# ConvFFN entry of a two-layer decoder trunk: matmuls of the first block alternate between gate and up, the norm's factor is taken earlier, and two operand tiles lie 384 bytes further on

## The chip, the cores and the metric

The kernel runs on one core of a Trainium2 chip. The metric is the device time of one execution in microseconds; the median of the runs is given, and beside it one execution that the hardware profiler recorded. Engines are called as the profile calls them: PE is TensorE (matmuls; PEld are its weight loads), DVE is VectorE, ACT is ScalarE, POOL is GpSimd, SP is SyncE, which issues the DMAs.

## The reference

Two layers over 256 tokens of width 1024. Each layer is attention, then a gated ConvFFN; cut to what matters here:

```python
def hybrid_layer(x, ...):
    h = rms_norm(x, ln1)
    proj = h @ w_in                       # 14 pieces, three kinds of attention heads
    ...
    x = x + jnp.concatenate([o_a, o_b, o_c], axis=-1) @ w_out
    return x + conv_ffn(rms_norm(x, ln2), w_gate, w_up, conv_w, conv_b, w_down)

def conv_ffn(h, w_gate, w_up, conv_w, conv_b, w_down):   # D_FF = 2816
    g = h @ w_gate
    u = h @ w_up
    g = conv_general_dilated(g, conv_w, ...) + conv_b    # causal, depthwise, width 3
    return (jax.nn.silu(g) * u) @ w_down

def rms_norm(x, g):
    return x * lax.rsqrt(jnp.mean(x * x, axis=-1, keepdims=True) + EPS) * g
```

## The kernel before

**Precision.** Every large product is made of three matmuls (`mm3`, L216): both operands are split into a high part and the rest (`hi`, `lo` for weights; `hTh`, `hTl` for the normed input; `oh`, `ol` for the attention output; `aTh`, `aTl` for the FFN's inner activations), and high x high, rest x high and high x rest are summed in PSUM. All of them here have 128 x 128 weights and 256 moving columns, one per token. The weight split (`split_next`, L194) costs one instruction on ACT (`hi`, L202) and one on DVE (`lo`, L203) per 128 x 1024 piece; the pieces come in a fixed order from the DMA queue of SP through three buffers `raw`, and their split parts go through a ring of seven buffers. `weights(ahead)` returns the next split piece and first splits so many pieces further on.

**The output projection and the entry to the ConvFFN.** The projection `w_out` is summed in eight PSUM accumulators (`ps_out`); its last two of eight pieces run behind one another (`down(acc, oT, 6, 8, ...)`), and as each of the eight output slices j is done, DVE adds it to the residual `xT` (L905), ACT makes `hTh[j]` and the square of the slice, DVE makes `hTl[j]`, and POOL adds the square into `sqs`. The FFN then goes in 22 blocks m of 128 inner channels; a block has 24 matmuls for gate and 24 for up, eight slices k of three matmuls each. The gain of the norm is in `hTh`; its factor R, one number per token, is applied later, to the gate product (`gate`, L935) and to the silu (L951). `norm2` (L919) makes R: `sqs` is split in two (`sqh` on ACT, `sql` on DVE), two matmuls with ones (`onesr`) sum it over the partitions into `ps_R`, and `rsqrt` (L221) makes R of the sum by one DVE, two ACT and three DVE instructions.

**What sets the order.** The DMA queue runs in written order throughout. In the loop over m, DVE, ACT and POOL are in written order too, `tc.manual_schedule(engines={ET.DVE, ET.Activation, ET.Pool})`; PE is ordered by a scheduler. At m = 0 the kernel before calls `weights()` twice with six pieces ahead, so that four further pieces (for blocks 2 and 3) are split before `norm2` is written. The gate and up accumulators of blocks take turns over three pairs of PSUM banks: a pair is used again three blocks later. The inner products then go to `w_down` (`ps_dn`) in the same manner, 22 x 24 matmuls.

**Where operands lie.** In a partition's memory each weight slice of `hi` and `lo` starts at a multiple of 512 bytes. `hTh`, `hTl`, `aTh`, `aTl`, `sqh` and `sql` start 448 bytes past one (a slice of 256 columns is 1024 bytes, so all slices do), `oh` and `ol` 64 bytes past one, `onesr` 448 past one. In the input projection (`ps_in`) the roles are exchanged: the moving columns are those of `hi` and `lo`, the weights those of `hTh` and `hTl`. In the piece of 256 columns (chunk 7) the moving operand therefore starts at a multiple of 512 and the weights 448 past one, which is the same distance, 64, as that of `oh` to its weights.

Of the kernel before, what the change touches and what calls it, by code (L numbers as in the profile page):

```python
# [23 lines left out]
D = 1024  # L24
HD = 64
DFF = 2816
NM = DFF // P
DEPTH = 2
EPS = 1e-6
# [29 lines left out]
CN = [len(c) for c in CHUNKS]  # L59
# [52 lines left out]
def emit(ctx, tc, a):  # L112
    nc = tc.nc
    V, A, T, G = nc.vector, nc.scalar, nc.tensor, nc.gpsimd

    cst = ctx.enter_context(tc.tile_pool(name="cst", bufs=1))
    lay = ctx.enter_context(tc.tile_pool(name="lay", bufs=2))
    wr = ctx.enter_context(tc.tile_pool(name="wr", bufs=3))
# [9 lines left out]
    ident = con[:, O_ID:O_ID + P]  # L128
    xT = cst.tile([P, 8, S], F32, name="xT")
    ones = cst.tile([P, P], F32, name="ones")  # L130
    onesr = cst.tile([P, P], F32R, name="onesr")
    G.memset(ones, 1.0)
    G.memset(onesr.bitcast(F32), 1.0)
    blk = [cst.tile([P, 16, 32], F32, name=f"blk{i}") for i in range(2)]
# [12 lines left out]
    def f(t):  # L147
        return t.bitcast(F32)
# [7 lines left out]
    for L in range(DEPTH):  # L156
        for c in range(8):
            n = CN[c]
# [17 lines left out]
    splits = []  # L176
    after = []

    raw0 = wr.tile([P, 4 * 2 * CN[0]], F32, name="raw0", bufs=1)

    def fetch(u):
        if u in raws:
# [8 lines left out]
        for load in extras.get(u, ()):  # L191
            load()

    def split_next():  # L194
        u, h = parts[len(ready)]
        src, n, np_ = stream[u]
        if h == 0:
            fetch(u)
        hi = wr.tile([P, 1024], F32R, tag="hi", name="hi", bufs=SPN)
        lo = wr.tile([P, 1024], F32R, tag="lo", name="lo", bufs=SPN)  # L200
        r = raws[u][:, h * n:(h + 1) * n]
        splits[:] = [A.activation(out=hi[:, :n], in_=r, func=ACTF.Copy),  # L202
                     V.tensor_tensor(out=lo[:, :n], in0=r, in1=f(hi[:, :n]), op=ALU.subtract)]  # L203
        ready.append((hi, lo))

    def weights(ahead=AHEAD):
        i = taken[0]
        taken[0] += 1
        while len(ready) < min(i + 1 + ahead, len(parts)):
            with ExitStack() as st:  # L210
                for ins in after:
                    st.enter_context(tc.issue_after(ins.ins))
                split_next()
        return ready[i]

    def mm3(out, lh, ll, rh, rl, start, stop, skip=False):  # L216
        T.matmul(out, lhsT=lh, rhs=rh, start=start, stop=False, skip_group_check=skip)  # L217
        T.matmul(out, lhsT=lh, rhs=rl, start=False, stop=False, skip_group_check=skip)  # L218
        T.matmul(out, lhsT=ll, rhs=rh, start=False, stop=stop, skip_group_check=skip)  # L219

    def rsqrt(out, ss, n, tmp=None):  # L221

        v, w, q = tmp or [sml.tile(list(out.shape), F32, tag=f"rs_{i}", name=f"rs_{i}") for i in "vwq"]

        V.tensor_scalar(v, ss, 1.0 / n, EPS, ALU.mult, ALU.add)
        A.activation(out=w, in_=v, func=ACTF.Ln)
        A.activation(out=w, in_=w, func=ACTF.Exp, scale=-0.5)
        V.tensor_tensor(q, w, w, ALU.mult)
        V.scalar_tensor_tensor(q, q, -0.5, v, ALU.mult, ALU.mult)
        V.scalar_tensor_tensor(out, q, 1.5, w, ALU.add, ALU.mult)  # L230
# [54 lines left out]
        nc.sync.dma_start(out=con[:, o0:o1], in_=a["con"][:, o0:o1])  # L285

    pools = []
    masks = cst.tile([P, 4, 384], BF16, name="masks")

    def load_masks(i):  # L290
        raw = pools[0].tile([P, 768], F32, tag="pr", name="raw_m", bufs=4)
# [53 lines left out]
    for L in range(DEPTH):  # L345
# [564 lines left out]
        with ExitStack() as ph:  # L910
            ff = ph.enter_context(tc.tile_pool(name=f"ff{L}", bufs=2, reuse_waits="tile"))

            aTh = ff.tile([P, 96 + NM * S], F32R, tag="aTh", name="aTh", bufs=1)[:, 96:].rearrange("p (m s) -> p m s", m=NM)
            aTl = ff.tile([P, NM, S], F32R, tag="aTl", name="aTl", bufs=1)
            cw = sm[:, O_CW:O_CW + 66].rearrange("p (m w) -> p m w", w=3)
            cb = sm[:, O_CB:O_CB + 22]
            R = lay.tile([P, S], F32, tag="R", name="R", bufs=1)

            def norm2():  # L919

                ps = bank("pt", "ps_R")
                sq, = sqs2
                sh, sl = [ff.tile([P, S], F32R, tag=n, name=n, bufs=1) for n in ("sqh", "sql")]
                A.copy(sh, sq)
                V.tensor_tensor(sl, sq, f(sh), ALU.subtract)
                for i, s_ in enumerate((sh, sl)):
                    T.matmul(ps[:, :S], lhsT=onesr, rhs=s_, start=i == 0, stop=i == 1)
                v, w, q = [ff.tile([P, S], F32, tag=n, name="R_" + n, bufs=3) for n in ("gr", "cy", "cs")]
                rsqrt(R, ps[:, :S], D, (v, w, q))

            gates, ups, ys, ss = {}, {}, {}, {}

            def gate(m):
                gr = ff.tile([P, S], F32, tag="gr", name="gr", bufs=3)
                V.tensor_tensor(gr, gates.pop(m), R, ALU.mult)  # L935
                return gr

            def conv(m, gr):
                y = ys[m] = ff.tile([P, S], F32, tag="cy", name="cy", bufs=3)
                A.activation(out=y, in_=gr, func=ACTF.Identity, scale=cw[:, m, 2:3], bias=cb[:, m:m + 1])  # L940

            def taps(m, gr):
                y = ys[m]
                for j in (1, 2):
                    V.scalar_tensor_tensor(out=y[:, j:], in0=gr[:, :S - j], scalar=cw[:, m, 2 - j:3 - j], in1=y[:, j:],  # L945
                                           op0=ALU.mult, op1=ALU.add)

            def silu(m):
                s_ = ss[m] = ff.tile([P, S], F32, tag="cs", name="cs_", bufs=3)
                A.activation(out=s_, in_=ys[m], func=ACTF.Silu)  # L950
                G.tensor_tensor(s_, s_, R, ALU.mult)  # L951

            def product(m):
                V.tensor_tensor(ys[m], ups.pop(m), ss.pop(m), ALU.mult)


            with tc.manual_schedule(engines={ET.DVE, ET.Activation, ET.Pool}):
                for m in range(NM + 2):
                    a_, b_, c_ = 2 <= m <= NM, m >= 2, m < NM
                    if a_:  # L960
                        gr = gate(m - 1)
                    if b_:
                        product(m - 2)
                    if c_:
                        gates[m], ups[m] = [bank((("acc", "s"), ("o", "m"))[m % 3 == 1][i], "ps_gu")[:, :S] for i in range(2)]
                        ws = [weights()]
                    if a_:
                        conv(m - 1, gr)
                    if b_:
                        A.copy(aTh[:, m - 2], ys[m - 2])  # L970
                    if a_:
                        taps(m - 1, gr)
                    if b_:
                        V.tensor_tensor(aTl[:, m - 2], ys[m - 2], f(aTh[:, m - 2]), ALU.subtract)
                    if c_:
                        ws.append(weights())
                    if a_:
                        silu(m - 1)
                    if c_:
                        for ps, (hi, lo) in zip((gates[m], ups[m]), ws):  # L980
                            for k in range(8):
                                cs = slice(k * P, (k + 1) * P)
                                mm3(ps, hi[:, cs], lo[:, cs], hTh[:, k], hTl[:, k], k == 0, k == 7)
                    if m == 0:
                        after.clear()
                        norm2()
                    if m == 1:
                        gr = gate(0)
                        conv(0, gr)
                        taps(0, gr)  # L990
                        silu(0)
                    if m in (10, 13) and L + 1 < DEPTH:
                        T1, T2 = rope_tables(L + 1, (m // 13,), None if m == 10 else (T1, T2))
            acc = [bank(t, "ps_dn") for t in ("pt", "pt", "o", "m")]
            for m in range(NM - 4):
                if m == 8 and L + 1 < DEPTH:
                    tc.keep_in_program_order(A.preload_act_table_set(TABLES))
                down(acc, (aTh, aTl), m, m + 1, NM - 1)
            if L + 1 < DEPTH:
                sqs1 = []  # L1000

            def new_x(j, ps):
                if L + 1 < DEPTH:
# [50 lines left out]
```

## Time and profile before

| | |
|---|---|
| median of 3 runs (656.75, 650.28, 649.35) | 650.28 us |
| the profiled execution | 650.62 us |
| its span, first to last instruction | 648.9 us |
| PE busy | 637.4 us (98%) |
| PE weight loads busy | 597.0 us (92%) |
| DVE busy | 473.6 us (73%) |
| ACT busy | 413.7 us (64%) |
| granted TensorE clock, mean | 1.000 |

Matmuls are pipelined: each is shown as lasting some 0.28 us, but the next starts after 0.11 to 0.12 us, so the pace is read from the starts. The entry to the ConvFFN of the first layer is at 146 to 160 us, that of the second at 464 to 478 us. A window of time counts the instructions that run in it, so one that began before its start is counted too.

### The profile page before, as it was taken

What the parts mean: (1) busy time and instruction counts of PE and PEld (TensorE: products, weight loads), DVE (VectorE), ACT (ScalarE), POOL (GpSimd) and SP (SyncE); (2) the same over time, 40 slices, a digit from 0 to 9 for tenths busy, and PEclk for the clock granted to TensorE, in tenths of its full rate; (3) what the DMA queues carried; (4) which work ended last, traced back from release to release, by engine and by line L of the source; (5) the groups of instructions that cost most, each with busy time, mean ns of one, the idle gap of its engine ahead of it and who ended that gap; (6) DMA issues with size and microseconds to landing.
All of it is one profiled execution on the core that took longest, in us unless ns stands there. A gap on an engine that the chain in (4) does not pass through costs nothing.

```text
span 648.9 us, 12854 instructions
## 1 busy us (share of the span) xinstructions
PE 637.4 (98%) x5074; PEld 597.0 (92%) x5074; DVE 473.6 (73%) x1024; ACT 413.7 (64%) x834; POOL 107.4 (17%) x123
## 2 busy tenths in 40 slices
PE   8999999999999999999999999999999999999997
PEld 8889878789999999999997887788999999999997
DVE  6679987758898888744487898685779888886432
ACT  7477899766775555543475789897757655555320
POOL 3301000012324422200120000010303222221000
PEclk9999999999999999999999999999999999999999
DMA  8853263434465555554664523333156655555501
GB/s 318 361 182 145 66 212 114 145 131 148 179 234 214 192 195 190 182 203 158 231 227 146 179 66 131 131 130 130 66 195 220 234 195 196 195 196 195 191 5 66
DMA packets 19356, 111.84 MB, mean 172 GB/s; under 512 B 2144, under 2 KB 3936, under 8 KB 8288
## 3 DMA queue, kind: packets, MB, share of 16 engines
q1 hardware_dynamic: 19296, 111.02, 48.0%
q8 instruction: 40, 0.66, 0.4%
q14 instruction: 20, 0.16, 0.1%
HBM read 109.97 MB, written 1.05 MB: 171 GB/s over the span
## 4 chain that ended last, share of the span: by engine, by line
PE 81%; DVE 8%; ACT 6%; DMA 2%; issue 2%; POOL 1%; SPq 0%; POOLq 0%; DVEq 0%; ACTq 0%
PE ps_gu L218 12%; PE ps_gu L219 12%; PE ps_gu L217 12%; PE ps_dn L218 6%; PE ps_dn L217 6%; PE ps_dn L219 6%; PE ps_in L217 4%; PE ps_in L218 4%; PE ps_in L219 4%; DVE lo L203 2%; PE ps_p L526 2%; PE ps_o L538 2%; ACT hi L202 2%; PE ps_out L217 2%; PE ps_out L219 2%
## 5 line engine op out<-in xcount | busy, mean ns | idle before, releaser
L203 DVE TENSOR_TENSOR lo<-raw,hi 128x1024 fp32r<-128x1024 f32 (+3 forms) x212 | 241.4, 1147 | 78.3 <-ACT hi L202 77.5
L202 ACT ACTIVATE hi<-raw 128x1024 fp32r<-128x1024 f32 (+3 forms) x212 | 208.3, 994 | 130.3 <-PE ps_gu L218 60.8
L218 PE MATMUL ps_gu<-hTl,hi 128*128 128x256 f32 x704 | 194.7, 277 | 0.2
L217 PE MATMUL ps_gu<-hTh,hi 128*128 128x256 f32 x704 | 194.5, 276 | 0.0
L219 PE MATMUL ps_gu<-hTh,lo 128*128 128x256 f32 x704 | 194.5, 276 | 0.0
L218 PEld LDWEIGHTS ps_gu<-hTl,hi 128*128 128x128 f32 x704 | 132.2, 188 | 0.6 <-DVE hTl L236 0.6
L219 PEld LDWEIGHTS ps_gu<-hTh,lo 128*128 128x128 f32 x704 | 132.2, 188 | 0.0
L217 PEld LDWEIGHTS ps_gu<-hTh,hi 128*128 128x128 f32 x704 | 132.2, 188 | 0.0
L219 PE MATMUL ps_dn<-aTh,lo 128*128 128x256 f32 x352 | 97.2, 276 | 0.0
L217 PE MATMUL ps_dn<-aTh,hi 128*128 128x256 f32 x352 | 97.2, 276 | 0.0
L218 PE MATMUL ps_dn<-aTl,hi 128*128 128x256 f32 x352 | 97.2, 276 | 0.0
L217 PE MATMUL ps_in<-hi,hTh 128*128 128x384 f32 (+3 forms) x256 | 88.2, 347 | 0.5 <-ACT vd L403 0.3
L218 PE MATMUL ps_in<-lo,hTh 128*128 128x384 f32 (+3 forms) x256 | 88.0, 344 | 0.7 <-DVE lo L203 0.7
L219 PE MATMUL ps_in<-hi,hTl 128*128 128x384 f32 (+3 forms) x256 | 88.0, 344 | 0.0
L219 PEld LDWEIGHTS ps_dn<-aTh,lo 128*128 128x128 f32 x352 | 66.1, 188 | 0.0
L217 PEld LDWEIGHTS ps_dn<-aTh,hi 128*128 128x128 f32 x352 | 66.1, 188 | 0.0
L218 PEld LDWEIGHTS ps_dn<-aTl,hi 128*128 128x128 f32 x352 | 66.1, 188 | 0.0
L217 PEld LDWEIGHTS ps_in<-hi,hTh 128*128 128x128 f32 x256 | 47.9, 188 | 6.5 <-issue 1.9
L218 PEld LDWEIGHTS ps_in<-lo,hTh 128*128 128x128 f32 x256 | 48.2, 188 | 4.3 <-DVE lo L203 1.1
L219 PEld LDWEIGHTS ps_in<-hi,hTl 128*128 128x128 f32 x256 | 48.2, 188 | 3.5 <-issue 0.9
L945 DVE SCALAR_TENSOR_TENSOR cy<-gr,sm,cy 128x255 f32<-128x255 f32 x88 | 42.5, 482 | 2.9 <-ACT cy L940 1.3
L217 PE MATMUL ps_out<-oh,hi 128*128 128x256 f32 x128 | 36.6, 289 | 0.0
(321 smaller groups left out, 922.4 us busy)
## 6 DMA issues: line engine op xcount, KB each, us to landing
raw<-w_gu SPq DMA_DIRECT2D x44, 1024.0 KB, 4.8
raw<-w_down SPq DMA_DIRECT2D x22, 1024.0 KB, 4.6
raw<-w_in SPq DMA_DIRECT2D x16, 768.0 KB, 4.5
raw<-w_in SPq DMA_DIRECT2D x8, 1024.0 KB, 4.7
raw<-w_out SPq DMA_DIRECT2D x8, 1024.0 KB, 4.8
w<-cw SPq DMA_DIRECT2D x4, 1024.0 KB, 10.7
raw<-w_in SPq DMA_DIRECT2D x4, 512.0 KB, 3.7
raw<-w_in SPq DMA_DIRECT2D x4, 274.0 KB, 5.1
```

Source lines behind the costliest of these rows:

```text
L202: splits[:] = [A.activation(out=hi[:, :n], in_=r, func=ACTF.Copy), V.tensor_tensor(out=lo[:, :n], in0=r, in1=f(hi[:, :n]), op=ALU.subtract)]
L203: V.tensor_tensor(out=lo[:, :n], in0=r, in1=f(hi[:, :n]), op=ALU.subtract)]
L217: T.matmul(out, lhsT=lh, rhs=rh, start=start, stop=False, skip_group_check=skip)
L218: T.matmul(out, lhsT=lh, rhs=rl, start=False, stop=False, skip_group_check=skip)
L219: T.matmul(out, lhsT=ll, rhs=rh, start=False, stop=stop, skip_group_check=skip)
L526: T.transpose(ps[:, i * P:(i + 1) * P], pr[:, i * P:(i + 1) * P], ident)
L538: return T.matmul(O[k * HD:(k + 1) * HD, qs], lhsT=vs[k][j], rhs=pTs[k][:, 256 * j:256 * j + 256 - 128 * j], start=first and j == 0, stop= ...
L945: V.scalar_tensor_tensor(out=y[:, j:], in0=gr[:, :S - j], scalar=cw[:, m, 2 - j:3 - j], in1=y[:, j:], op0=ALU.mult, op1=ALU.add)
```

## The change

1. In block 0 the products are written k by k, gate and up in turn (`products`), where before all eight k of gate came first and then those of up; later blocks keep gate first.
2. PE is in written order in this loop as well. The two matmuls of `norm2` stand behind the 48 of block 0; the scheduler had put them in between the matmuls of block 1.
3. `norm2` is written around two weight splits: `sqh` right behind the `hi` of the first, `sql` ahead of its `lo`; the first DVE and both ACT instructions of the factor between `hi` and `lo` of the second. Block 0 splits nothing further ahead (`weights(0)`), and later blocks keep four pieces ahead, not six. R is done before any further split.
4. ACT's function table for silu is loaded behind the factor's last ACT instruction, not ahead of the first silu. The gate work of block 0 (`gate(0)`, `conv`, `taps`, `silu`) moves up between the splits of block 1's turn.
5. Tiles are padded: `oh` and `ol` lie 896 bytes further on, which is 384 past a multiple of 512, so that they now start 448 bytes past one. `onesr` now starts at a multiple of 512. Everything else moves by 512 or 1024 bytes, or has no part in these matmuls.

```diff
-    onesr = cst.tile([P, P], F32R, name="onesr")
+    onesr = cst.tile([P, 2 * P], F32R, name="onesr")[:, 16:16 + P]
...
-    raw0 = wr.tile([P, 4 * 2 * CN[0]], F32, name="raw0", bufs=1)
+    raw0 = wr.tile([P, 4 * 2 * CN[0] + 32], F32, name="raw0", bufs=1)
...
-    def split_next():
+    def split_next(between=None):
...
-        splits[:] = [A.activation(out=hi[:, :n], in_=r, func=ACTF.Copy),
-                     V.tensor_tensor(out=lo[:, :n], in0=r, in1=f(hi[:, :n]), op=ALU.subtract)]
+        splits[:] = [A.activation(out=hi[:, :n], in_=r, func=ACTF.Copy)]
+        if between:
+            between()
+        splits.append(V.tensor_tensor(out=lo[:, :n], in0=r, in1=f(hi[:, :n]), op=ALU.subtract))
...
-    masks = cst.tile([P, 4, 384], BF16, name="masks")
+    masks = cst.tile([P, 4 * 384 + 192], BF16, name="masks")[:, :4 * 384].rearrange("p (a b) -> p a b", a=4)
...
+                def total():
+                    A.copy(sh, sq)
+                    V.tensor_tensor(sl, sq, f(sh), ALU.subtract)
+                    for i, s_ in enumerate((sh, sl)):
+                        T.matmul(ps[:, :S], lhsT=onesr, rhs=s_, start=i == 0, stop=i == 1)
+                def first_value():
+                    V.tensor_scalar(v, ps[:, :S], 1.0 / D, EPS, ALU.mult, ALU.add)
+                    A.activation(out=w, in_=v, func=ACTF.Ln)
+                    A.activation(out=w, in_=w, func=ACTF.Exp, scale=-0.5)
+                    A.preload_act_table_set("silu_and_others")
...
+                    split_next(total)
+                after.clear()
+                split_next(first_value)
+                V.tensor_tensor(q, w, w, ALU.mult)
+                V.scalar_tensor_tensor(q, q, -0.5, v, ALU.mult, ALU.mult)
+                V.scalar_tensor_tensor(R, q, 1.5, w, ALU.add, ALU.mult)
...
+            def products(m, ws):
+                order = [(k, i) for k in range(8) for i in range(2)] if m == 0 else [(k, i) for i in range(2) for k in range(8)]
+                for k, i in order:
+                    (hi, lo), cs = ws[i], slice(k * P, (k + 1) * P)
+                    mm3((gates, ups)[i][m], hi[:, cs], lo[:, cs], hTh[:, k], hTl[:, k], k == 0, k == 7)
...
-            with tc.manual_schedule(engines={ET.DVE, ET.Activation, ET.Pool}):
+            with tc.manual_schedule(engines={ET.DVE, ET.Activation, ET.Pool, ET.PE}):
...
+                    if m == 0:
+                        products(0, [weights(0) for _ in range(2)])
+                        norm2()
+                    else:
+                        gr = gate(m - 1) if m <= NM else None
...
+                            ws.append(weights(4))
```

**PE, the start of block 0** in layer 0; `ps_gu_1917` is gate, `ps_gu_1918` up. Before:

```order
L219 MATMUL ps_out_1485<-oh_901,lo_1531 128x256
L217 MATMUL ps_gu_1917<-hTh_91,hi_1612 128x256
L218 MATMUL ps_gu_1917<-hTl_92,hi_1612 128x256
L219 MATMUL ps_gu_1917<-hTh_91,lo_1613 128x256
L217 MATMUL ps_gu_1917<-hTh_91,hi_1612 128x256
L218 MATMUL ps_gu_1917<-hTl_92,hi_1612 128x256
L219 MATMUL ps_gu_1917<-hTh_91,lo_1613 128x256
```

Now:

```order
L221 MATMUL ps_out_1485<-oh_901,lo_1531 128x256
L219 MATMUL ps_gu_1917<-hTh_91,hi_1612 128x256
L220 MATMUL ps_gu_1917<-hTl_92,hi_1612 128x256
L221 MATMUL ps_gu_1917<-hTh_91,lo_1613 128x256
L219 MATMUL ps_gu_1918<-hTh_91,hi_1679 128x256
L220 MATMUL ps_gu_1918<-hTl_92,hi_1679 128x256
L221 MATMUL ps_gu_1918<-hTh_91,lo_1680 128x256
```

Each slice k is now used by six matmuls in a row, so the last slice, k = 7, is first read 42 matmuls after the start, where it was 21.

**PE, the norm's two matmuls.** `hi_1750` and `lo_1751` belong to the gate of block 1. Before:

```order
L218 MATMUL ps_gu_2005<-hTl_92,hi_1750 128x256
L927 MATMUL ps_R_1989<-sqh_1990,onesr_76 128x256
L219 MATMUL ps_gu_2005<-hTh_91,lo_1751 128x256
...
L217 MATMUL ps_gu_2005<-hTh_91,hi_1750 128x256
L927 MATMUL ps_R_1989<-sql_1991,onesr_76 128x256
L218 MATMUL ps_gu_2005<-hTl_92,hi_1750 128x256
```

Now:

```order
L221 MATMUL ps_gu_1918<-hTh_91,lo_1680 128x256
L933 MATMUL ps_R_1967<-sqh_1968,onesr_76 128x256
L933 MATMUL ps_R_1967<-sql_1969,onesr_76 128x256
L219 MATMUL ps_gu_1994<-hTh_91,hi_1750 128x256
L220 MATMUL ps_gu_1994<-hTl_92,hi_1750 128x256
```

Both stand one behind the other between block 0 and block 1, and apart from block 0 nothing else has changed place on PE.

**DVE, from the last `hTl` to the first product.** Before:

```order
L236 SCALAR_TENSOR_TENSOR hTl<-xT,sm,hTh 128x256 x2
L203 TENSOR_TENSOR lo<-raw,hi 128x1024 x4
L925 TENSOR_TENSOR sql<-sqs,sqh 128x256
L225 TENSOR_SCALAR R_gr<-ps_R 128x256
L228 TENSOR_TENSOR R_cs<-R_cy 128x256
L229 SCALAR_TENSOR_TENSOR R_cs<-R_cs,R_gr 128x256
L230 SCALAR_TENSOR_TENSOR R<-R_cs,R_cy 128x256
L203 TENSOR_TENSOR lo<-raw,hi 128x1024 x2
L935 TENSOR_TENSOR gr<-ps_gu,R 128x256
```

Now:

```order
L238 SCALAR_TENSOR_TENSOR hTl<-xT,sm,hTh 128x256 x2
L931 TENSOR_TENSOR sql<-sqs,sqh 128x256
L205 TENSOR_TENSOR lo<-raw,hi 128x1024
L936 TENSOR_SCALAR R_gr<-ps_R 128x256
L205 TENSOR_TENSOR lo<-raw,hi 128x1024
L947 TENSOR_TENSOR R_cs<-R_cy 128x256
L948 SCALAR_TENSOR_TENSOR R_cs<-R_cs,R_gr 128x256
L949 SCALAR_TENSOR_TENSOR R<-R_cs,R_cy 128x256
L955 TENSOR_TENSOR gr<-ps_gu,R 128x256
L205 TENSOR_TENSOR lo<-raw,hi 128x1024
```

Four splits stood ahead of `sql` and six ahead of the first `gr`; now it is none and two.

## Rows read from the trace of the kernel before

**Rows 1.** The page's chain that ended last, shares of the span by engine

```profile
PE 81%; DVE 8%; ACT 6%; DMA 2%; issue 2%; POOL 1%; SPq 0%; POOLq 0%; DVEq 0%; ACTq 0%
```

**Rows 2.** Windows, PE: stretch, us, busy us (count), granted clock, DMA share, GB/s

```profile
155.40:327.30 171.90, 171.90 (x1519) 1.00 0.55 196
473.40:644.90 171.50, 171.50 (x1515) 1.00 0.48 173
138.16:146.39 8.23, 8.23 (x71) 1.00 0.36 127
456.14:464.37 8.23, 8.23 (x71) 1.00 0.37 128
105.03:108.79 3.76, 3.76 (x34) 1.00 0.00 0
113.56:115.81 2.25, 2.25 (x22) 1.00 0.48 127
```

**Rows 3.** Timeline of PE, first layer's entry: start, duration, instruction

```profile
146.52 0.28 PE L217 MATMUL ps_gu<-hTh,hi 128*128 128x256 f32 x1
...
148.99 0.28 PE L217 MATMUL ps_gu<-hTh,hi 128*128 128x256 f32 x1
149.39 0.38 PE L218 MATMUL ps_gu<-hTl,hi 128*128 128x256 f32 x1
149.61 0.28 PE L219 MATMUL ps_gu<-hTh,lo 128*128 128x256 f32 x1
...
152.67 0.28 PE L218 MATMUL ps_gu<-hTl,hi 128*128 128x256 f32 x1
152.89 0.39 PE L927 MATMUL ps_R<-sqh,onesr 128*128 128x256 f32 x1
153.12 0.28 PE L219 MATMUL ps_gu<-hTh,lo 128*128 128x256 f32 x1
...
154.81 0.39 PE L927 MATMUL ps_R<-sql,onesr 128*128 128x256 f32 x1
155.03 0.28 PE L218 MATMUL ps_gu<-hTl,hi 128*128 128x256 f32 x1
...
158.67 0.28 PE L217 MATMUL ps_gu<-hTh,hi 128*128 128x256 f32 x1
```

**Rows 4.** Timeline of PE, second layer: first matmul of block 0 and of block 2

```profile
464.50 0.28 PE L217 MATMUL ps_gu<-hTh,hi 128*128 128x256 f32 x1
...
476.63 0.28 PE L217 MATMUL ps_gu<-hTh,hi 128*128 128x256 f32 x1
```

**Rows 5.** Timeline of DVE, first layer's entry

```profile
147.82 1.51 DVE L236 SCALAR_TENSOR_TENSOR hTl<-xT,sm,hTh 128x256 fp32r<-128x256 f32 x2
149.73 4.68 DVE L203 TENSOR_TENSOR lo<-raw,hi 128x1024 fp32r<-128x1024 f32 x4 [0.40 <-ACT hi L202]
154.34 0.41 DVE L925 TENSOR_TENSOR sql<-sqs,sqh 128x256 fp32r<-128x256 f32 x1
155.23 0.42 DVE L225 TENSOR_SCALAR R_gr<-ps_R 128x256 f32<-128x256 f32 x1 [0.48 <-PE ps_R L927]
160.12 0.42 DVE L935 TENSOR_TENSOR gr<-ps_gu,R 128x256 f32<-128x256 f32 x1
164.86 0.42 DVE L954 TENSOR_TENSOR cy<-ps_gu,cs__2071 128x256 f32<-128x256 f32 x1 [2.31 <-POOL cs__2071 L951]
```

**Rows 6.** Timeline of ACT, first layer's entry

```profile
148.66 3.89 ACT L202 ACTIVATE hi<-raw 128x1024 fp32r<-128x1024 f32 x4
152.45 0.39 ACT L924 CAST sqh<-sqs 128x256 fp32r<-128x256 f32 x1
162.30 1.28 ACT L950 ACT_TABLE_LOAD   x1 [1.12 <-DVE cy L945]
```

**Rows 7.** Timeline of POOL: the last four additions into sqs

```profile
146.47 3.45 POOL L246 TENSOR_TENSOR sqs<-sqs,xsq 128x256 f32<-128x256 f32 x4
```

**Rows 8.** The page's DMA issues: the FFN's weights, KB each, us to landing

```profile
raw<-w_gu SPq DMA_DIRECT2D x44, 1024.0 KB, 4.8
```

More of the change, by code (lines that the diff above doesn't have):

```diff
@@ L923, in norm2 @@
                 sh, sl = [ff.tile([P, S], F32R, tag=n, name=n, bufs=1) for n in ("sqh", "sql")]
[L924 to L927, printed above, removed]
                 v, w, q = [ff.tile([P, S], F32, tag=n, name="R_" + n, bufs=3) for n in ("gr", "cy", "cs")]
-                rsqrt(R, ps[:, :S], D, (v, w, q))
+                def total():
[8 more added lines that the diff above has]
+                    A.preload_act_table_set("silu_and_others")
+                with ExitStack() as st:
+                    for ins in after:
+                        st.enter_context(tc.issue_after(ins.ins))
+                    split_next(total)
[4 more added lines that the diff above has]
+                V.scalar_tensor_tensor(R, q, 1.5, w, ALU.add, ALU.mult)
             gates, ups, ys, ss = {}, {}, {}, {}
@@ L954, in product @@
                 V.tensor_tensor(ys[m], ups.pop(m), ss.pop(m), ALU.mult)
-            with tc.manual_schedule(engines={ET.DVE, ET.Activation, ET.Pool}):
-                for m in range(NM + 2):
[L959 to L964, printed above, removed]
-                        gates[m], ups[m] = [bank((("acc", "s"), ("o", "m"))[m % 3 == 1][i], "ps_gu")[:, :S] for i in range(2)]
[L966 to L983, printed above, removed]
@@ new lines, in products @@
+            def products(m, ws):
[4 more added lines that the diff above has]
+            with tc.manual_schedule(engines={ET.DVE, ET.Activation, ET.Pool, ET.PE}):
+                for m in range(NM + 2):
+                    if m < NM:
+                        gates[m], ups[m] = [bank((("acc", "s"), ("o", "m"))[m % 3 == 1][i], "ps_gu")[:, :S] for i in range(2)]
@@ L984, in emit @@
                     if m == 0:
-                        after.clear()
+                        products(0, [weights(0) for _ in range(2)])
                         norm2()
[L987 to L991, printed above, removed]
+                    else:
+                        gr = gate(m - 1) if m <= NM else None
+                        if m >= 2:
+                            product(m - 2)
+                        ws = []
+                        if m == 1:
+                            conv(0, gr)
+                        if m < NM:
+                            ws.append(weights(4))
+                        if 2 <= m <= NM:
+                            conv(m - 1, gr)
+                        if m >= 2:
+                            A.copy(aTh[:, m - 2], ys[m - 2])
+                        if m <= NM:
+                            taps(m - 1, gr)
+                        if m == 1:
+                            silu(0)
+                        if m >= 2:
+                            V.tensor_tensor(aTl[:, m - 2], ys[m - 2], f(aTh[:, m - 2]), ALU.subtract)
+                        if m < NM:
+                            ws.append(weights(4))
+                        if 2 <= m <= NM:
+                            silu(m - 1)
+                        if m < NM:
+                            products(m, ws)
```

## The prediction

> **What bounds the kernel now.** I read the chain of waits first: 81% of what ended last is PE, so time is won where PE waits or runs slower than it can [rows 1]. Then windows of PE at several places, to get its pace from the count of starts. In the long stretch from the entry of the first layer's ConvFFN to the end of its `ps_dn`, 1,519 matmuls run in 171.90 us; two of them began before the window, so 171.90 / 1,517 = 0.1133 us each, and the second layer's stretch gives the same (171.50 / 1,513) [rows 2]. There PE waits for nothing, so no work of DVE, ACT or the queues counts there. In each layer 70 of the last starts of `ps_out` (one of the 71 was under way) take 8.23 us, 0.1176 us each [rows 2], with the same 256 columns and the granted clock at 1.00 in both, the 2.4 GHz level. So there are two paces without any wait, 0.1133 (fast) and 0.1177 (slow), 4.4 ns apart.
>
> Last I read the entry itself. From the first matmul of block 0 to the first of block 2 there are 98 matmuls, and they take 158.67 - 146.52 = 12.15 us in the first layer [rows 3] and 476.63 - 464.50 = 12.13 in the second [rows 4]. At the fast pace 98 would take 11.11, at the slow one 11.53. The loss sits in three places [rows 3]: `hTl` of slice 7 is awaited (0.40 from 148.99 to 149.39, then 0.22 to the next), and each of the two `ps_R` matmuls costs about 0.2 us in starts that are 0.22 apart; between the first stop and the second PE runs at the slow pace, 26 starts from 149.61 to 152.67, 0.1177 each.
>
> **The change part by part.**
>
> *Slice by slice in block 0.* `hTl` of slice 7 is done at 147.82 + 1.51 = 149.33 [rows 5]. It is now first read 42 matmuls after the block's start, 42 x 0.1133 = 4.8 us, so at 151.0 or later even if PE starts 0.3 us sooner. The wait goes, with 1.6 us to spare. No other slice is nearer: six matmuls last 0.68 to 0.71 us, one turn of DVE's `xT` and `hTl` takes about 0.9, so the margin only shrinks towards k = 7.
>
> *The norm's two matmuls.* They now stand 48 matmuls behind the start, at about 151.7. `sqs` is complete at 146.47 + 3.45 = 149.92 [rows 7]; `sqh` takes 0.39 on ACT, which has one split (0.97) before it instead of four (3.89) [rows 6]; `sql` takes 0.41 on DVE, which has no split before it instead of four (4.68) [rows 5]. So both are there by 150.8, 0.9 us ahead of PE. What is late next is nothing on PE: `R_gr` follows 0.42 us after the second matmul, at 152.2 instead of 155.23; then one split (1.2), then the three further DVE steps at about 0.42; the first `gr` comes near 155.3 instead of 160.12 [rows 5].
>
> *What hangs on the other engines.* Two splits stand behind `gr` that used to stand before it. I estimate the pieces of block 3 done near 158.7 and 162.4; PE reads them at 146.2 + 146 x 0.1133 = 162.7 and 2.7 later. The product of block 0, at 164.86 before, comes near 163.2, and block 3's up, which takes over its bank, starts at 165.4. The table load (1.28 [rows 6]) moves into the time in which ACT waits for R. With four pieces ahead in place of six the `raw` buffers come free later, so their DMAs are issued later. They land in 4.8 us [rows 8] and two blocks, 2 x 48 x 0.1133 = 10.9 us, remain. Nothing moves on the DMA queue itself. All of this I cost at 0 because PE's work of those blocks covers it; the thinnest cover is 2 to 3 us.
>
> Sum for the entry: 12.15 + 12.13 - 2 x 11.11 = 2.06 us saved at the fast pace, 24.28 - 2 x 11.53 = 1.2 at the slow one.
>
> *The 384 bytes.* No row shows `oh` at its new distance from the weights. Its old distance, 64 bytes, occurs once more, in the 256-column piece of the input projection, and that runs slow as well: 32 starts in 3.76 us, 0.1175 each [rows 2]. The products at distance 448, `ps_gu` and `ps_dn`, run fast for 1,517 starts together. That is the ground for taking the new place as fast: (0.1177 - 0.1133) x 72 x 2 = 0.63 us in the two undisturbed stretches, and at most 0.0044 x 120 x 2 = 1.06 us in the rest of `ps_out`, which is cut up by waits for the attention; I take a third, 0.35. Bounds: 0 to 1.69. The rule is not strict, since `ps_out` ran 20 starts fast at the old distance, 2.25 us from 113.56 on [rows 2], and `ps_gu` the 26 slow ones at the good one [rows 3]: a pace once taken goes on until PE is stopped. The lower bound can fall below zero through that; it is the rival on the other side, below.
>
> Sum: 2.06 + 0.63 + 0.35 = 3.0 us. The profiled execution took 650.62, so 647.6 of it remain; the median of the three runs is 0.34 lower, which gives 647.2. **Forecast: 647.4 us.**
>
> **The rivals.**
>
> *A: the place of `oh` does nothing.* Then `ps_out` stays slow, block 0 starts at that pace and keeps it, and only the stops are saved: 1.2 us, 649.2. For it: 26 slow starts at distance 448. Against it: the agreement of three products with their distances. The Trainium skill is on this rival's side. Its page "TensorE: Matmul & The Clock Gate", section "Part 2: What happens when you issue a matmul", says that TensorE reads the moving operand and the next weights through two separate SBUF ports, so that loading weights takes no bandwidth from the running matmul. By that rule the 384 bytes would be worth 0 and the time 649.2; the two paces at one shape, size and clock are not explained by it.
>
> *B: slower, PE stays at the slow pace.* In the kernel before, PE is stopped three times in each entry, and the fast pace of the next 1,517 matmuls begins behind the last of these stops. Now no stop is left between the end of the attention and the end of the layer's `ps_dn`. If PE enters block 0 slow, nothing that the trace shows would end it: 1,517 x 0.0044 = 6.7 us more per layer. One layer gives 647.4 + 6.7 + the lost gains of that layer (about 0.9), 655.0; both give 662.6. It decides from about 270 slow matmuls on (1.2 / 0.0044), six blocks, where the saving of the stops is used up. For it: the paces carry over from `ps_in` to `ps_out` and from `ps_out` to `ps_gu`; and one run of the kernel before took 656.75, 6.5 to 7.4 above the other two, the price of one layer at the slow pace (an inference, no trace of that run is there). Against it: behind stops at distance 448 the fast pace came up more often than not.
>
> *C: a new wait.* If `sqs` or a split comes 0.9 us later than I have it, PE stops at `ps_R` again, in both layers; or a split of block 3 is late by more than its 3 us. Up to 1 us per layer: 648.5 to 650. Against it: every step's duration is in the rows. That the matmuls are in written order is plain from the listing, so "it doesn't do what it says" has no share of its own.
>
> **How the numbers follow.** Forecast 0.60, A 0.14, B 0.19 (one layer 0.13, both 0.06), C 0.07. The forecast's own range: 650.28 less all bounds (2.06 + 1.69) is 646.5, and with 0.5 for the spread of runs 646.0; upwards 649. The 8-in-10 range takes in A and C up to 651.0 and leaves out B: 646.0 to 651.0. Differences of 2%, 13 us, are about what counts as measured. No case reaches 637, so faster by over 2% gets 0.01. Slower by over 2% is above 663.3: B in both layers ends just below it, so it needs that and a little more, 0.03. Within 2%: 0.96.
>
> **What would show it.** In the changed profile: 98 matmuls from block 0 to block 2 in 11.1 us in each layer (11.5 if slow), no start in block 0 or at `ps_R` more than 0.13 apart; `R_gr` near 152 and the first `gr` near 155; the last stretch of `ps_out` at 0.1133. A `ps_out` at 0.1177 with a fast `ps_gu` speaks for A without B; a window of 100 us in `ps_gu` with 850 matmuls instead of 883 is B. A stop at `ps_R`, or a stop of PE in blocks 2 to 5 for a split or a bank, is C and would show my cover wrong.

## The result

The changed kernel takes 647.23 us, median of 18 runs between 646.61 and 648.08; a second series of 11 has the median 647.25 (646.55 to 648.02). The forecast was 647.4 with a range of 646.0 to 651.0.

The kernel before, run beside it, had a median of 656.68, not 650.28. Over all series it ran 70 times. One run took 895.65; no trace of it is there, and it is left out. The other 69 stand on three levels:

| level | runs of the kernel before | runs of the changed kernel |
|---|---|---|
| 649.35 to 650.93 (changed: 646.55 to 648.08) | 33 | 29 |
| 656.0 to 657.4 | 30 | 0 |
| 662.9 to 663.4 | 6 | 0 |

So the ratio of the times depends on which levels fell into the series: 0.9886 [0.9861, 0.991] in the first, 0.9941 [0.9914, 0.9968] in the second; the first leaves out the three runs of the highest level. Both are inside 2%, "the same" by that measure, and both are clearly below 1. The profile shown ahead of the prediction was one of the lowest level; against that level the change is worth 3 us, against the middle one 9.4, against the highest 16.

### The profile page after: what moved, and what is told of

It reads as the page before. It is cut to its first block, busy times and chain, and to the rows that moved or that the text cites. A ratio compares the mean times of both kernels' runs of the same rounds, so it can differ in the third digit from the quotient of the medians.

```text
span 645.9 us, 12816 instructions
## 1 busy us (share of the span) xinstructions
PE 634.5 (98%) x5074; PEld 595.2 (92%) x5074; DVE 469.5 (73%) x1024; ACT 414.6 (64%) x834; POOL 105.1 (16%) x123
## 3 DMA queue, kind: packets, MB, share of 16 engines
HBM read 109.97 MB, written 1.05 MB: 172 GB/s over the span
## 4 chain that ended last, share of the span: by engine, by line
PE 86%; ACT 5%; DVE 5%; issue 2%; POOL 1%; DMA 1%; SPq 0%; POOLq 0%; DVEq 0%; ACTq 0%
PE ps_gu L221 12%; PE ps_gu L220 12%; PE ps_gu L219 12%; PE ps_dn L220 6%; PE ps_dn L221 6%; PE ps_dn L219 6%; PE ps_in L219 5%; PE ps_in L221 5%; PE ps_in L220 5%; PE ps_o L541 2%; PE ps_p L529 2%; PE ps_out L219 2%; PE ps_out L221 2%; PE ps_out L220 2%; ACT hi L202 2%
## 5 line engine op out<-in xcount | busy, mean ns | idle before, releaser
L960 ACT ACTIVATE cy<-gr,sm 128x256 f32<-128x256 f32 x44 | 26.5, 603 | 43.8 <-DVE gr L955 43.8
```

## The profile after

From the page, the span and the chain of work that ended last, by engine:

```profile
span 645.9 us, 12816 instructions
...
PE 86%; ACT 5%; DVE 5%; issue 2%; POOL 1%; DMA 1%; SPq 0%; POOLq 0%; DVEq 0%; ACTq 0%
```

The span was 648.9 and the profiled execution 650.62; now they are 645.9 and 647.70. PE's share of the chain went from 81% to 86% [rows 1], and what DVE had there fell from 8% to 5%. PE has the same 5,074 matmuls in both traces; what went is waiting.

The entry of the first layer in the timeline of PE (start, duration, instruction), and the same two ends in the second layer:

```profile
146.58 0.28 PE L219 MATMUL ps_gu<-hTh,hi 128*128 128x256 f32 x1
...
152.02 0.28 PE L933 MATMUL ps_R<-sqh,onesr 128*128 128x256 f32 x1
152.13 0.28 PE L933 MATMUL ps_R<-sql,onesr 128*128 128x256 f32 x1
152.24 0.28 PE L219 MATMUL ps_gu<-hTh,hi 128*128 128x256 f32 x1
...
157.68 0.28 PE L219 MATMUL ps_gu<-hTh,hi 128*128 128x256 f32 x1
...
462.62 0.28 PE L219 MATMUL ps_gu<-hTh,hi 128*128 128x256 f32 x1
...
473.72 0.28 PE L219 MATMUL ps_gu<-hTh,hi 128*128 128x256 f32 x1
```

98 matmuls take 157.68 - 146.58 = 11.10 us, and 473.72 - 462.62 = 11.10, where it was 12.15 and 12.13 [rows 3, 4]. The three gaps of [rows 3] are gone, and the norm's two matmuls start 0.11 apart like all others.

The output projection in the timeline of PE: its first matmul in both layers, and in the first layer the start from which its last stretch runs at the fast pace:

```profile
109.33 0.28 PE L219 MATMUL ps_out<-oh,hi 128*128 128x256 f32 x1
...
138.76 0.28 PE L219 MATMUL ps_out<-oh,hi 128*128 128x256 f32 x1
...
426.58 0.29 PE L219 MATMUL ps_out<-oh,hi 128*128 128x256 f32 x1
```

From 138.76 to the first `ps_gu` at 146.58 there are 69 starts, 0.1133 each; it was 0.1176 [rows 2]. The first matmuls of `ps_out` in the trace before:

```profile
108.92 0.28 PE L217 MATMUL ps_out<-oh,hi 128*128 128x256 f32 x1
...
428.05 0.28 PE L217 MATMUL ps_out<-oh,hi 128*128 128x256 f32 x1
```

Up to block 0 the whole of `ps_out` takes 146.58 - 109.33 = 37.25 and 462.62 - 426.58 = 36.04 now; before it took 37.60 and 36.45.

The long stretches that answer to the first two lines of [rows 2] (columns as there), each as long as there and moved up with the entry:

```profile
155.00:326.90 171.90, 171.90 (x1519) 1.00 0.56 200
471.00:642.50 171.50, 171.50 (x1514) 1.00 0.50 177
```

The counts are 1,519 and 1,514 where they were 1,519 and 1,515, at the same granted clock. The pace of the FFN has not changed against the run whose trace was read. What changed, going by the times, is that it is reached in both layers in all 29 runs.

DVE and ACT at the first layer's entry, and POOL's last line there, in the order of the engines:

```profile
148.03 1.51 DVE L238 SCALAR_TENSOR_TENSOR hTl<-xT,sm,hTh 128x256 fp32r<-128x256 f32 x2
150.62 0.42 DVE L931 TENSOR_TENSOR sql<-sqs,sqh 128x256 fp32r<-128x256 f32 x1 [1.07 <-ACT sqh L930]
...
152.44 0.42 DVE L936 TENSOR_SCALAR R_gr<-ps_R 128x256 f32<-128x256 f32 x1 [0.27 <-PE ps_R L933]
...
155.29 0.42 DVE L955 TENSOR_TENSOR gr<-ps_gu,R 128x256 f32<-128x256 f32 x1
157.34 1.22 DVE L205 TENSOR_TENSOR lo<-raw,hi 128x1024 fp32r<-128x1024 f32 x1 [1.62 <-ACT hi L202]
...
161.25 1.23 DVE L205 TENSOR_TENSOR lo<-raw,hi 128x1024 fp32r<-128x1024 f32 x1 [1.77 <-ACT hi L202]
...
162.73 0.41 DVE L974 TENSOR_TENSOR cy<-ps_gu,cs__2010 128x256 f32<-128x256 f32 x1
```

```profile
150.18 0.41 ACT L930 CAST sqh<-sqs 128x256 fp32r<-128x256 f32 x1 [0.26 <-POOL sqs L248]
...
153.79 1.28 ACT L939 ACT_TABLE_LOAD   x1
```

```profile
144.08 6.07 POOL L248 TENSOR_TENSOR sqs<-sqs,xsq 128x256 f32<-128x256 f32 x7 [26.15 <-ACT xsq L246]
```

`hTl` of the last slice is there at 149.54, 1.9 us ahead of its reader (the 44th start, about 151.45). `sqs` ends at 150.15 and is now what `sqh` waits for; `sql` ends at 151.04, 1.1 ahead of its matmul. `R_gr` moved from 155.23 to 152.44, the first `gr` from 160.12 to 155.29 [rows 5], and the table load from 162.30 [rows 6] to 153.79, into the time in which ACT has nothing to do.

## The experiments

The trace before had left one thing unexplained: the two paces at one shape and one clock. The theory that went into the runs was that the pace depends on where the operands lie and that PE keeps a pace once it has it. The rival was that the reordering alone, through fewer stops, does it, or that the place does nothing.

**The new order with `oh` and `ol` back at 64.**

```diff
-    raw0 = wr.tile([P, 4 * 2 * CN[0] + 32], ...)
+    raw0 = wr.tile([P, 4 * 2 * CN[0]], ...)
...
-    masks = cst.tile([P, 4 * 384 + 192], BF16, ...)[:, :4 * 384]...
+    masks = cst.tile([P, 4, 384], BF16, name="masks")
```

(The padding of `raw0` makes up for that of `masks`, so that the weights behind both stay at a multiple of 512; the two go together.)

> The changed kernel with oh and ol back at 64 bytes past a multiple of 512 (masks and raw0 unpadded); PE's order and onesr as changed. Theory 'place and memory' (the distance of moving operand to weights decides which pace PE falls into, and the pace then goes on until PE is stopped): the last stretch of ps_out at 0.1177 us a start, block 0 entered slow, no stop left, so ps_gu and ps_dn stay slow in both layers: 647.2 + 0.8 (ps_out) + 2 x 6.9 = about 662 in most runs. Rival 'the stops alone' (without stops PE is fast, wherever oh lies): 647 to 649, ps_gu at 0.1133. Rival 'place does nothing for ps_out, pace is chance': a mixture of 648, 655 and 662.

661.98 us, 6 runs between 661.37 and 662.28. Windows of PE inside `ps_gu` of both layers:

```profile
170.00:260.00 90.00, 90.00 (x766) 1.00 0.57 203
490.00:575.00 85.00, 85.00 (x724) 1.00 0.57 200
```

The same windows of the changed kernel itself:

```profile
170.00:260.00 90.00, 90.00 (x796) 1.00 0.58 208
490.00:575.00 85.00, 85.00 (x752) 1.00 0.58 206
```

Two of each count began before the window: 90 / 764 = 0.1178 against 90 / 794 = 0.1133, at a granted clock of 1.00 in all four lines. With `oh` at 64 the last stretch of `ps_out` is slow, PE comes into block 0 slow, and now that nothing stops it there it stays so to the end of `ps_dn`, in both layers of the trace and, by the times, in all six runs. So 384 bytes in two tiles are worth 14.75 us in the new order. The Trainium skill, page "TensorE: Matmul & The Clock Gate", section "Part 2: What happens when you issue a matmul", has weights and moving columns read through two ports that do not take from each other; with that alone the 384 bytes would be worth nothing, and the measurement decides against leaving it at that.

**The old order with all three paddings** (the kernel before with the `onesr`, `raw0` and `masks` lines of the change).

```diff
+    onesr = cst.tile([P, 2 * P], F32R, name="onesr")[:, 16:16 + P]
...
+    raw0 = wr.tile([P, 4 * 2 * CN[0] + 32], ...)
...
+    masks = cst.tile([P, 4 * 384 + 192], BF16, ...)[:, :4 * 384]...
```

> The kernel before with all three paddings of the change (oh and ol at 448, onesr at 0) and nothing else. Place and memory: the last stretch of ps_out is fast (0.6 to 0.8 us saved in all), but PE is still stopped three times in each entry, and the pace behind the last stop is drawn again: runs at about 649, 656 and 662, as the kernel before has them less 0.7. Rival 'the old place of oh or onesr was the whole cause': all runs at 649, none above 651.

12 runs: 7 between 649.02 and 650.12, 5 between 655.98 and 656.97; against the kernel before 0.9988 [0.9941, 1.0035]. The three stops are back. Timeline of PE, second layer, the matmuls that follow a gap:

```profile
465.75 0.39 PE L218 MATMUL ps_gu<-hTl,hi 128*128 128x256 f32 x1 [0.26 <-DVE hTl L236]
469.26 0.38 PE L927 MATMUL ps_R<-sqh,onesr 128*128 128x256 f32 x1
...
471.16 0.39 PE L927 MATMUL ps_R<-sql,onesr 128*128 128x256 f32 x1
```

PE enters block 0 fast in both layers of the trace, and still 5 of 12 runs are on the level that is one slow layer higher. Expected were runs on the third level too; none of the 12 is there. Good places alone do not keep the fast pace over a stop.

**The changed kernel with block 0's gate first**, which brings one of the stops back, the wait for `hTl`.

```diff
-                order = [(k, i) for k in range(8) for i in range(2)] if m == 0 else [...]
+                order = [(k, i) for i in range(2) for k in range(8)]
```

> The changed kernel with block 0 written gate first, then up, so that hTl of slice 7 is awaited 21 matmuls in. Place and memory: one stop in each entry, 0.3 to 0.4 us each (647.9 without more), and behind the stop the pace is drawn again, with no later stop to end a slow one: runs at 648, 655 and 661. Rival 'a stop costs only its own length': 647.9 in all runs, within 0.5.

12 runs: 5 between 648.15 and 649.15, 7 between 654.68 and 656.06. The profiled execution is one of the latter and shows both outcomes of the same stop. PE, first layer and second:

```profile
149.10 0.28 PE L219 MATMUL ps_gu<-hTh,hi 128*128 128x256 f32 x1
149.64 0.39 PE L220 MATMUL ps_gu<-hTl,hi 128*128 128x256 f32 x1 [0.26 <-DVE hTl L238]
149.87 0.29 PE L221 MATMUL ps_gu<-hTh,lo 128*128 128x256 f32 x1
...
472.69 0.28 PE L219 MATMUL ps_gu<-hTh,hi 128*128 128x256 f32 x1
473.23 0.39 PE L220 MATMUL ps_gu<-hTl,hi 128*128 128x256 f32 x1 [0.26 <-DVE hTl L238]
473.45 0.28 PE L221 MATMUL ps_gu<-hTh,lo 128*128 128x256 f32 x1
```

The gap is 0.54 in both. Behind it the windows of `ps_gu` read

```profile
170.00:260.00 90.00, 90.00 (x767) 1.00 0.58 204
490.00:575.00 85.00, 85.00 (x752) 1.00 0.60 214
```

slow in the first layer, fast in the second. Where PE comes out fast twice, the two stops cost 1.5 us together (the five runs have the median 648.70, against 647.23); one that ends slow costs 6.6 more (655.33, median of the seven). This is the only trace of a run on a middle level; of the kernel before and of the old order with the paddings none was kept, so that their upper levels are slow layers too is inferred from the same price.

**The changed kernel with `onesr` back at 448.**

```diff
-    onesr = cst.tile([P, 2 * P], F32R, name="onesr")[:, 16:16 + P]
+    onesr = cst.tile([P, 2 * P], F32R, name="onesr")[:, :P]
```

> The changed kernel with onesr back at 448 past a multiple of 512, so that the norm's two matmuls have distance 0 between moving operand and weights. Place and memory, if two matmuls are enough to change the pace: some layers slow, runs at 654 or 661 among 647. If a pace goes on through two matmuls at another distance: 647.2 in all runs, within 0.5. Costs of its own: none over 0.1 us.

660.81 us, 6 runs between 660.54 and 662.12. PE at the end of block 0:

```profile
151.35 0.28 PE L221 MATMUL ps_gu<-hTh,lo 128*128 128x256 f32 x1
151.47 0.28 PE L933 MATMUL ps_R<-sqh,onesr 128*128 128x256 f32 x1
151.59 0.28 PE L933 MATMUL ps_R<-sql,onesr 128*128 128x256 f32 x1
151.70 0.28 PE L219 MATMUL ps_gu<-hTh,hi 128*128 128x256 f32 x1
```

Up to 151.47, the first of the two, the starts are 0.1133 apart on the mean, and 0.1178 from there on. PE has not waited for anything. The 48 matmuls of block 0 ran fast; two matmuls with weights at 448 turned PE slow, and 1,536 matmuls with good places behind them did not turn it back. 64 bytes of one tile that is read four times in the whole kernel are worth 13.6 us.

**The moving operand's place scanned in `ps_dn`.** The slices of `aTh` and `aTl` are put 1,088 bytes apart instead of 1,024, so that the place moves on by 64 bytes with every block; once in the changed kernel, once with `onesr` at 448 besides, so that `ps_dn` is entered slow.

```diff
-    aTh = ff.tile([P, 96 + NM * S], ...)[:, 96:]...
+    aTh = ff.tile([P, 96 + NM * (S + 16) + 32], ...)[:, 96:96 + NM * (S + 16)]...[:, :, :S]
...
```

> The changed kernel with the inner activations aTh and aTl stored 1088 bytes apart instead of 1024, so that in ps_dn the distance of moving operand to weights grows by 64 bytes with each block: 448 in block 0, 0 in block 1, 64, 128, ... 384 in block 7, 448 again in block 8, and so on; 24 matmuls each. ps_gu is unchanged and arrives fast. If the distance sets the pace: block 0 at 0.1133, the turn to 0.1177 within a few matmuls of a block at a bad distance (0 by the run with the old onesr), and back to 0.1133 only where some distance takes PE out of the slow pace; the pattern repeats every 8 blocks. Rival 'what made PE slow at the norm's two matmuls was something else of theirs than the distance': ps_dn stays at 0.1133 throughout, 647.2.

> The same scan of distances in ps_dn, entered slow: onesr is at its old place, so that ps_gu runs at 0.1177 from the norm's two matmuls on. If some distance takes PE out of the slow pace without a stop, the same blocks as in the scan from fast turn to 0.1133, and from there on both scans read alike. If none does: ps_dn at 0.1177 throughout, about 661.

652.71 and 662.02 us, one run each. Entered fast, block 0 (place 448) runs at 113.3 ns, and the next block, at place 0, slows down within its first matmuls, in both layers. PE there in the first:

```profile
268.82 0.28 PE L221 MATMUL ps_dn<-aTh,lo 128*128 128x256 f32 x1
268.94 0.28 PE L219 MATMUL ps_dn<-aTh,hi 128*128 128x256 f32 x1
...
269.64 0.28 PE L219 MATMUL ps_dn<-aTh,hi 128*128 128x256 f32 x1
269.76 0.28 PE L220 MATMUL ps_dn<-aTl,hi 128*128 128x256 f32 x1
```

The first matmul of the new place starts at 268.94; from there starts are 0.117 apart (0.70 for six, to 269.64), then 0.12. Blocks 4, 8, 12 and 16 lie at 192 or 448 again, and none gets the fast pace back; the second layer, entered behind the attention's stops, starts fast again. Place 0 is the only one that was entered at the fast pace, so the scan does not say whether the others would end it. The means of the slow blocks up to block 17 in both kernels (the last four run slice by slice, mixed), in ns by place modulo 512: 117.8 at 192 and 448, 118.0 at 64 and 320, 118.5 at 128 and 384, 119.6 at 0 and 256. The slow pace of places 256 bytes apart is equal.

**Everything shifted by 128 bytes** in the changed kernel: weights at 128, moving operands at 64, `onesr` at 128. All distances between operands stay as they are.

```diff
-    con = cst.tile([P, O_MK], F32, name="con")
+    con = cst.tile([P, O_MK + 32], F32, name="con")
```

> The changed kernel with every tile moved on by 128 bytes (con is padded): weights now start 128 past a multiple of 512, hTh, hTl, oh, ol, aTh, aTl 64 past one; all distances are as in the change. If the distance counts: 647.2 within 0.5, ps_gu and ps_dn at 0.1133. If the place of one operand by itself counts (64 past a multiple was the old place of oh): ps_out slow and some or all layers at 0.1177, 654 to 662.

661.89 us, 4 runs between 661.59 and 662.19; `ps_gu` has 767 and 724 matmuls in the windows used above, 0.1176 us each, as with `oh` at 64. This is the time that was expected if the place counts. But `ps_gu` and `ps_dn` are not tested by it: between the last stretch of `ps_out` and the end of `ps_dn` nothing stops PE, so they carry on the pace at which that one stretch ended, and it ended slow in both layers. In the first layer, a window of PE there:

```profile
138.40:146.50 8.10, 8.10 (x71) 1.00 0.35 129
```

Two began before it: 8.10 / 69 = 0.1174. Whether the two places allow the fast pace is read where PE starts anew behind a wait, and that is in the cut-up part of `ps_out`. There the shifted kernel does run fast; one stretch in PE's timeline:

```profile
127.51 0.28 PE L220 MATMUL ps_out<-ol,hi 128*128 128x256 f32 x1
...
129.55 0.28 PE L220 MATMUL ps_out<-ol,hi 128*128 128x256 f32 x1
```

These are 18 starts in 2.04 us, 0.1133 each. In the profiled execution of every kernel, `ps_out` has 13 stretches of ten or more matmuls without a gap, both layers together. Judged by their last five starts, 9 of the 13 end fast in the shifted kernel (moving operand at 64, weights at 128), 8 to 10 in the nine executions with the places of the change (448 and 0), and 2 and 1 in the kernel before and the first experiment (64 and 0). So with the distance kept the fast pace comes as often as in the change, at other places: this run does not refute the distance. What it changes is which stretch ends fast. In all nine executions with the places of the change the last stretch but one is slow and the last one fast, in both layers; here it is the other way round, and only the last one is handed on to the FFN. Why they swap, no run shows.

**Only the inner activations at 192, and only the weights at 64.**

```diff
-    aTh = ff.tile([P, 96 + NM * S], ...)[:, 96:]...
-    aTl = ff.tile([P, NM, S], ...)
+    aTh = ff.tile([P, 32 + NM * S], ...)[:, 32:]...
+    aTl = ff.tile([P, NM * S + 64], ...)[:, :NM * S]...
```

```diff
+    pad = sml.tile([P, 112], F32, tag="pad", name="pad", bufs=1)
+    G.memset(pad, 0.0)
-    raw0 = wr.tile([P, 4 * 2 * CN[0] + 32], ...)
+    raw0 = wr.tile([P, 4 * 2 * CN[0] + 48], ...)
```

> The changed kernel with the inner activations aTh and aTl (the moving operand of ps_dn) at 192 past a multiple of 512 bytes instead of 448; nothing else moves. Theory: places count modulo 256 bytes, since in the scan the slow pace of places 256 bytes apart was equal (117.8 for 448 and 192). Then ps_dn stays at 0.1133 us per matmul and the time at about 647.2. Rival: only 448 is good. Then ps_dn turns slow at its first matmuls in both layers, 2 x 528 x 0.0044 = 4.6 us, about 652.

> The changed kernel with all split weights (hi and lo) at 64 past a multiple of 512 bytes instead of 0; the moving operands of ps_out, ps_gu and ps_dn stay at 448, onesr at 0. Theory: the weights' place counts too (onesr at 448 turned PE slow while the moving operand was at 448). Then no product of the FFN finds the fast pace in either layer, about 662. Rival: only the moving operand's place counts, and what onesr did at 448 is that it lay at the moving operand's own place. Then ps_out's last stretch, ps_gu and ps_dn stay at 0.1133 and the time at about 647.2.

647.26 and 665.84 us, one run each. A window of PE in the first, `ps_dn` of the first layer (two or three of the count began before it):

```profile
268.00:324.00 56.00, 56.00 (x497) 1.00 0.57 196
```

56 / 495 = 0.1131: 192 is as good as 448. In the second, `ps_gu`, whose moving operand never left 448:

```profile
170.00:260.00 90.00, 90.00 (x761) 1.00 0.60 201
490.00:575.00 85.00, 85.00 (x719) 1.00 0.62 209
```

90 / 759 = 0.1186 and 85 / 717 = 0.1186. `ps_gu` carries on the pace of `ps_out` here too, but in this kernel not one of the 13 stretches of `ps_out` ends fast, with a moving operand that never left 448. So the moving operand's place alone does not decide; the weights' place counts as well. Two readings of it are left. Either the fast pace wants the moving operand at 192 and the weights at 0, both modulo 256 bytes, or it wants a distance (moving operand less weights) of 192 modulo 256. The fast stretches of the shifted kernel, at 64 and 128, are for the distance; its slow last stretches are what a theory of the distance alone leaves open. The size of the slow pace does go by the distance: 118.66 ns here (384), 118.5 in the scan at 384, 117.8 at the distance 448 wherever it lay. The run is 3.8 us above the expected 662; 2 x 1,584 x 0.86 ns = 2.7 of them are this slower slow pace.

**The input projection at the good places too.** Its weights `hTh` and `hTl` are put at 0 for the first norm only, and its moving operand at 192 in all pieces below 512 columns.

```diff
+    hIn, hFf = [[t[:, o:o + 8 * S]... for t in hts] for o in (16, 0)]
+        if n < 1024:
+            hi, lo = hi[:, 48:48 + n], lo[:, 48:48 + n]
```

> The changed kernel with the input projection at the good places too: pieces of fewer than 512 columns (14 of 16 chunks) have their split weights, there the moving operand, 192 bytes past a multiple of 512, and the normed input of the first norm, there the weights, lies at a multiple of 512; for ps_gu it lies at 448 as before. Theory: moving operand at 192 and weights at 0, both modulo 256 bytes, is the pair that allows the fast pace. In the changed kernel a 384-column ps_in takes mostly 173 to 174 ns and a 256-column one 117 to 118; at the fast pace 170 and 113.3, so at most 2 x (192 x 3.3 + 48 x 4.4) ns = 1.7 us where nothing waits; 645.5 to 646.7. Rival: the two 512-column chunks and the ones of 274 columns, which stay where they are, turn PE slow and the attention's own matmuls keep it so; nothing gained, 647.2.

> The changed kernel itself, once more beside the one above on the same chip: about 647.2 in every run, since no run of it so far was further than 1 us from that.

647.66 (647.12 to 648.24) against 647.25 (646.55 to 648.02), 11 runs each: no gain, rather 0.4 lost. One run of chunk 1 in the first layer, 384 columns, in the changed kernel, PE:

```profile
16.77 0.33 PE L221 MATMUL ps_in<-hi,hTl 128*128 128x384 f32 x1
...
22.31 0.34 PE L221 MATMUL ps_in<-hi,hTl 128*128 128x384 f32 x1
```

and with the places changed:

```profile
16.77 0.34 PE L223 MATMUL ps_in<-hi,hTl 128*128 128x384 f32 x1
...
22.42 0.34 PE L223 MATMUL ps_in<-hi,hTl 128*128 128x384 f32 x1
```

It is the same 32 starts: 5.54 / 32 = 0.1731 before the edit, 5.65 / 32 = 0.1766 after it. The 256-column chunk of that layer did go from 117.8 to 113.6 ns a start, but that is 35 matmuls, 0.14 us; in the second layer the same chunk stayed at 117.7. The starts of 384 columns, 317 in both layers without a gap, went from 173.5 to 175.5 ns on the mean, 0.6 us in all. So what is good for 256 columns was a little worse for 384, and no version here beats the changed kernel.

## Why the prediction was right, and where it was not

**The entry, 2.06 us: right.** It was to be 98 matmuls in 11.1 us per layer; 1.05 and 1.03 us were saved. The steps that hid the rest stood where they were put: the first `gr` near 155.3 (155.29), block 3's pieces near 158.7 and 162.4 (done at 158.56 and 162.48), block 0's product near 163.2 (162.73). `R_gr` came at 152.44, 0.2 later than said, because block 0 starts at 146.58 and not some 0.3 earlier than before: `ps_out` itself began 0.41 later, at 109.33 instead of 108.92.

**The 384 bytes of `oh`, 0.98: right in kind, 0.2 too high.** `ps_out` lost 37.60 - 37.25 = 0.35 and 36.45 - 36.04 = 0.41 us, 0.76 together. Some 0.6 of that are the two undisturbed stretches; the third of the cut-up part that was guessed at 0.35 gave about 0.15.

**The distance as the rule: not shown, and not refuted.** The prediction took the rule as a distance between operands, from three products that agreed with it. They were no test, because in the trace before the weights of all 256-column products but one lay at the same place, so that distance and place could not differ. The later runs agree with the distance as to which places let the fast pace come up (192 modulo 256, the shifted kernel's stretches of `ps_out` included), but with the distance kept and everything 128 bytes further on, the one stretch that the FFN hangs on ended slow and the time was 661.89. That the forecast took the new place as fast for this stretch is borne out; why it is fast is open.

**`onesr` had no term: missed.** The change moves it, the prediction costs it at nothing without saying so, and it is worth 13.6 us: with `onesr` at 448 the forecast mechanism (PE enters block 0 fast and nothing stops it) is undone by the norm's own two matmuls. The step "a pace once taken goes on until PE is stopped" held for the slow pace. The fast one can end without a stop: at `onesr`'s matmuls by the times in all six runs, and at place 0 in both layers of the scan, each time at distance 0. Not every bad distance ends it so: the 20 fast starts of `ps_out` in [rows 2] ran at distance 64.

**The terms were added, and they do not add.** The order with `oh` at 64 (and `onesr` at its new place) gives 661.98, all six runs between 661.37 and 662.28, worse than all but six of the 69 runs of before; the places alone give 0.9988 of before. Together they give 647.23. That 2.06 + 0.98 taken off 650.62 came out right was in part luck: the profiled execution of before happened to be fast in both layers, as fewer than half of its runs are, and the median of three happened to be one of those too.

**Rival B was the right mechanism in the wrong kernel.** It priced a slow layer at 6.7 us and gave 662.6 for two; the new order without the place costs 661.98, so the price was right. But it was put 0.19 on the changed kernel, and it is the kernel before that has one slow layer or two in 36 of 69 runs, if its upper levels are what their price says. The reading of the run of 656.75 as one such layer fits that; what was not drawn from it was that one in three is no rarity, and that a median of three can stand on one level of several. If each layer came out slow by itself with a chance of 0.30, 69 runs would fall 34, 29 and 6 on the three levels; they fell 33, 30 and 6. That fits a toss at the stops of each entry, but what tips it was not found: in the two layers of the gate-first kernel the stop looks alike to 0.01 us and ends differently. In the last two stretches of `ps_out` it is no toss: nine traces, two layers each, end them alike.

**Rival A fell, and C did not come.** No start from block 0 to the end of `ps_dn`, in either layer, is further than 0.13 from the one before it.

**What stays open.** Why the last stretch of `ps_out` ends fast with the places of the change (nine profiled executions, both layers, 18 of 18) and slow with everything 128 bytes further on, while behind the stops in block 0 either pace comes; whether the rule is a pair of places or a distance; and why there are two paces at all. A kernel with the distance kept in other steps than 128 bytes, and one with a stop at the head of `ps_dn`, were not tried.

## What to carry to other kernels

Where back-to-back matmuls of one shape show two paces at one granted clock, find where both operands start, modulo 256 bytes, and give every matmul of the stream the places that were seen to run fast, the rare ones too; two matmuls were enough to spoil a layer. A saved stop is then worth more than its own length, because a stop can end in the slow pace. Before a run is taken to rule a place out, look whether PE started anew there or only carried on the pace it came with. And when one of three runs is off by the price of one whole stage at another pace, take it for a second level of the kernel and get more runs before a profile of the other level is used as the base.

## What the runs showed of the hardware

- Two paces for a 128 x 128 x 256 matmul at a granted clock of 1.00: 113.3 ns, and 117.8 to 119.6 ns by the distance of the operands. The fast one was kept through the FFN only with the moving operand at 448 or 192 and the weights at 0 modulo 512. With the same distance at 64 and 128 it came up in 9 of 13 stretches of `ps_out`, at distance 64 in 1 and 2 of 13, at distance 384 in none.
- The slow pace outlasts its cause: 1,536 matmuls of good places behind two of a bad one stayed slow, and so did the good blocks of the scan.
- For 384 columns the moving operand at 192 and the weights at 0 gave 176.6 ns in one run of 32 starts, where moving operand at 0 and weights at 448 gave 173.1.
- The wait of a matmul for its operand costs more than the wait: the start that follows one is 0.22 to 0.23 behind it (149.64 to 149.87, 473.23 to 473.45), twice the usual.
